# Projections by Strassen's seven products, with intermediates in DRAM, in a hybrid SSD and gMLP layer on one core

## The chip, the cores and the metric

The kernel runs on one core of one Trainium2 chip. The metric is the device time of one execution in microseconds (us). Matmuls run on TensorE (PE), elementwise work on VectorE (DVE), ScalarE (ACT) and GpSimd (POOL); all DMA transfers are issued from the queue of SyncE (SP). Each engine works through its own instructions in the order in which the program holds them.

## The reference, cut to what matters

2048 tokens of width 1024, one layer, all in float32:

```python
h = rms_norm(x, pre_w)
proj = jnp.einsum('bld,dc->blc', h, w_in)               # 1024 -> 6160 columns
u, v, zg, z, xbc, dt_raw = jnp.split(proj, SPLITS, axis=-1)
y_a = spatial_gating(u, v, zg, v_norm_w, v_norm_b, ws, bs, gmlp_norm_w)
y_b = ssd_mixer(xbc, z, dt_raw, conv_w, conv_b, dt_bias, a_log, d_skip, ssd_norm_w)
y = jnp.concatenate([y_a, y_b], axis=-1)                # 2048 columns
...
# spatial_gating: per head and chunk of 128 tokens, u * (W_s v + b) * silu(zg), grouped RMS norm
# ssd_mixer: causal convolution of width 4 over xbc and SiLU, chunked scan with decay,
#   D skip, times silu(z), grouped RMS norm
# then y times w_out (2048 -> 1024), RMS norm, plus x
```

u, v, zg and z have 1024 columns each, xbc 2048, dt 16. The large products are h times w_in and y times w_out.

## The kernel before, in words

The tokens are worked through in four blocks of 512 (`block`, called for b = 0 to 3). For a block, the normalised input is held in SBUF as `hT`, channels on partitions, in two parts: a high part rounded to the format of the fast matmul and a low part, the remainder. Weights are split alike: `load_w` loads 128 rows of a weight unit, ACT makes the high part (L120), and DVE or, every third time, POOL subtracts it for the low part (L123). A product is then three matmuls (`mm3`, L127 to 130): high by high, high by low, low by high.

The projections of a block are cut into units of eight k-steps of 128 channels. A unit has four accumulators in PSUM, one bank each: four units z with 256 columns (the first 272, since dt's 16 columns ride along), four `xbc`, two `v`, two halves of `w_o` for the SSD's part of y, four `uz` (u and zg side by side), and two halves of `w_o` for the gating's part. All but z have 512 columns, so a unit is 8 x 4 x 3 = 96 matmuls. Every block loads all weights again, five k-steps ahead (`LOOK`).

Everything else is a task (`spawn`, `run_tasks`): a generator that emits a piece of work between two k-steps. After an `xbc` unit the task `ssd` does a head group: convolution (POOL L311, then DVE L313 three times), decay matrices `E` read from DRAM by broadcast (DVE L327), their product with C times B (L361), and per chunk of 128 tokens the scan (L364 to L395). `spatial` and `gating` do the gMLP branch. Results stay in SBUF: `hT`, z's gate `zs`, v, and y as `yT`, split again into two parts (L133, L134). The order on each engine comes from a scheduler that works over the emitted program.

Of the kernel before, what the change touches and what calls it, by code (L numbers as in the profile page):

```python
# [10 lines left out]
BF16 = mybir.dt.bfloat16  # L11
# [16 lines left out]
DTC = GC + NH    # columns of the first gate unit: z of group 0, then dt  # L28
# [7 lines left out]
def hybrid_kernel(ctx: ExitStack, tc: tile.TileContext, x, x_t, pre_w, w_v, w_uz, w_xbc, w_z0, w_z,  # L36
                  v_w, v_b, ws_t, bs_t, gn_w, conv_w, conv_b, dt_bias, a_log, d_skip, sn_w,
                  w_o, post_w, out):
    nc = tc.nc
    seq = x.shape[0]  # L40
    nb = seq // T

    const = ctx.enter_context(tc.tile_pool(name="const", bufs=1))
    hpool = ctx.enter_context(tc.tile_pool(name="hpool", bufs=1))
    ypool = ctx.enter_context(tc.tile_pool(name="ypool", bufs=8))
    t4 = ctx.enter_context(tc.tile_pool(name="t4", bufs=8))
    wraw = ctx.enter_context(tc.tile_pool(name="wraw", bufs=4))
# [6 lines left out]
    dram = ctx.enter_context(tc.tile_pool(name="dram", bufs=2, space=DRAM))  # L54
# [43 lines left out]
        # what b and bs add to the gated sum: rowsum(ws) * b + bs  # L98
# [8 lines left out]

    def row_weights(src):
# [76 lines left out]
    h_tiles = {}  # L185
# [512 lines left out]
```

## Time and profile before

| | |
|---|---|
| time, median of 3 runs | 1691.16 us (1688.84 to 1691.71) |
| profiled execution, its span | 1686.8 us |
| PE busy | 1640.3 us, 97% |
| DVE busy | 1030.1 us, 61% |
| ACT busy | 825.5 us, 49% |
| POOL busy | 793.9 us, 47% |
| PE's granted clock, mean | 0.996 of full speed |
| DMA | 191.91 MB, 114 GB/s mean |

The span runs from the first to the last instruction of the profiled execution; the time of a run lies a few us over it. An engine's busy share is an average over stages; a share of 97% means that this engine almost never waits, and the other engines' shares say how much room they have beside it.

### The profile page before, as it was taken

To read this page: it belongs to the slowest core of one execution; us is meant where nothing else is said; L and a number is where in the kernel's file an instruction comes from. 1 tells how busy PE (TensorE), PEld (TensorE's weight loads), DVE (VectorE), ACT (ScalarE), POOL (GpSimd) and SP (SyncE) were. 2 spreads that over 40 slices of the span, in tenths; PEclk is the share of its full clock that TensorE was granted. 3 is DMA by queue.
4 is the path that set the end of the run, shared out by engine and by line. 5 is a ranking of instruction groups with operands and counts; after the bars stand their busy time and mean duration, and the time that the engine had idled before them with its cause. 6 is when DMAs were issued, how large, how long until landed. Compare 5 with 4: busy or idle time off the path is not lost.

```text
span 1686.8 us, 24913 instructions
## 1 busy us (share of the span) xinstructions
PE 1640.3 (97%) x8554; PEld 1395.5 (83%) x8554; DVE 1030.1 (61%) x1938; ACT 825.5 (49%) x1725; POOL 793.9 (47%) x875
## 2 busy tenths in 40 slices
PE   6999999999999999999999999999999999999997
PEld 5888888887888878888788887888878888888886
DVE  5678772346767777234666787724467777862444
ACT  5456644354446654344444565434534556444442
POOL 4457643234546655233545666513344556551333
PEclk9999999999999999999999999999999999999999
DMA  6323443334433343324353334333524324333341
GB/s 225 98 91 97 130 124 112 92 107 134 154 102 91 110 127 124 107 88 138 95 161 104 88 119 132 125 98 90 155 80 156 112 76 124 91 93 106 89 137 70
DMA packets 111471, 191.91 MB, mean 114 GB/s; under 512 B 13552, under 2 KB 30192, under 8 KB 111344
## 3 DMA queue, kind: packets, MB, share of 16 engines
q1 hardware_dynamic: 111344, 190.32, 36.6%
q8 instruction: 67, 1.10, 0.3%
q14 instruction: 60, 0.49, 0.1%
HBM read 181.75 MB, written 8.52 MB: 113 GB/s over the span
## 4 chain that ended last, share of the span: by engine, by line
PE 80%; DVE 11%; POOL 3%; issue 3%; DMA 2%; ACT 2%; SPq 0%; DVEq 0%; POOLq 0%; ACTq 0%
PE acc L128 23%; PE acc L129 23%; PE acc L130 23%; DVE cv_out L313 3%; PE y_ps L378 2%; DVE E L327 2%; PE s_ps L440 2%; PE y_tp L413 2%; DVE h L234 2%; DMA E<-scr 2%; POOL cv_out L311 2%; PE y_ps L381 1%; PE st_ps L383 1%; PE cb_ps L351 1%; DVE w L123 1%
## 5 line engine op out<-in xcount | busy, mean ns | idle before, releaser
L120 ACT ACTIVATE w<-raw 128x512 fp32r<-128x512 f32 (+2 forms) x576 | 330.7, 580 | 477.7 <-PE acc L130 386.8
L123 POOL TENSOR_TENSOR w<-raw,w 128x512 fp32r<-128x512 f32 (+2 forms) x192 | 243.6, 1269 | 478.0 <-ACT w L120 430.3
L128 PE MATMUL acc<-w,hT 128*128 128x512 f32 (+2 forms) x1280 | 453.8, 357 | 4.7 <-ACT v L552 3.2
L130 PE MATMUL acc<-w,hT 128*128 128x512 f32 (+2 forms) x1280 | 451.2, 354 | 0.8 <-POOL hT L236 0.8
L129 PE MATMUL acc<-w,hT 128*128 128x512 f32 (+2 forms) x1280 | 448.2, 350 | 0.0
L123 DVE TENSOR_TENSOR w<-raw,w 128x512 fp32r<-128x512 f32 (+2 forms) x384 | 270.8, 711 | 267.5 <-ACT w L120 265.2
L128 PEld LDWEIGHTS acc<-w,hT 128*128 128x128 f32 x1280 | 244.0, 191 | 35.3 <-ACT v L552 4.5
L129 PEld LDWEIGHTS acc<-w,hT 128*128 128x128 f32 x1280 | 244.1, 191 | 30.1
L130 PEld LDWEIGHTS acc<-w,hT 128*128 128x128 f32 x1280 | 242.8, 190 | 31.2 <-POOL hT L236 1.1
L128 PE MATMUL acc<-hT,w 128*128 128x512 f32 x512 | 203.7, 398 | 0.0
L130 PE MATMUL acc<-hT,w 128*128 128x512 f32 x512 | 202.7, 396 | 0.0
L129 PE MATMUL acc<-w,yT 128*128 128x512 f32 x512 | 201.7, 395 | 0.0
L129 PE MATMUL acc<-hT,w 128*128 128x512 f32 x512 | 201.4, 393 | 0.0
L128 PE MATMUL acc<-w,yT 128*128 128x512 f32 x512 | 195.5, 395 | 0.3
L130 PE MATMUL acc<-w,yT 128*128 128x512 f32 x512 | 193.5, 391 | 0.0
L313 DVE SCALAR_TENSOR_TENSOR cv_out<-cv_raw,cw,cv_out 128x512 f32<-128x512 f32 x192 | 164.8, 888 | 24.1 <-POOL cv_out L311 23.9
L327 DVE TENSOR_SCALAR E<-E,cst 128x128 f32<-128x128 f32 x256 | 105.6, 470 | 67.1 <-DMA E<-scr 67.1
L128 PEld LDWEIGHTS acc<-w,yT 128*128 128x128 f32 x512 | 96.1, 188 | 22.3 <-DVE o L577 1.6
L129 PEld LDWEIGHTS acc<-w,yT 128*128 128x128 f32 x512 | 96.2, 188 | 21.1 <-DVE w L123 1.0
L130 PEld LDWEIGHTS acc<-hT,w 128*128 128x128 f32 x512 | 96.2, 188 | 20.1
L130 PEld LDWEIGHTS acc<-w,yT 128*128 128x128 f32 x512 | 96.3, 188 | 19.6
L128 PEld LDWEIGHTS acc<-hT,w 128*128 128x128 f32 x512 | 96.3, 188 | 19.3 <-ACT zs L542 0.4
(131 smaller groups left out, 2270.9 us busy)
## 6 DMA issues: line engine op xcount, KB each, us to landing
raw<-w_xbc SPq DMA_DIRECT2D x128, 256.0 KB, 2.8
raw<-w_o SPq DMA_DIRECT2D x128, 256.0 KB, 2.6
raw<-w_uz SPq DMA_DIRECT2D x128, 256.0 KB, 2.7
E<-scr SPq DMA_DIRECT2D x64, 256.0 KB, 3.4
raw<-w_v SPq DMA_DIRECT2D x64, 256.0 KB, 2.7
raw<-w_z SPq DMA_DIRECT2D x96, 128.0 KB, 2.0
xt<-x SPq DMA_DIRECT2D x32, 256.0 KB, 3.9
h<-x_t SPq DMA_DIRECT2D x32, 256.0 KB, 3.0
```

What stands on the lines that cost most here:

```text
L120: nc.scalar.activation(w[:, 0, :], raw, AF.Copy)
L123: eng.tensor_tensor(w[:, 1, :], raw, w[:, 0, :], ALU.subtract)
L128: nc.tensor.matmul(dst, lhsT=a_hi, rhs=b_hi, start=first, stop=False)
L129: nc.tensor.matmul(dst, lhsT=a_hi, rhs=b_lo, start=False, stop=False)
L130: return nc.tensor.matmul(dst, lhsT=a_lo, rhs=b_hi, start=False, stop=last)
L234: nc.vector.scalar_tensor_tensor(h, h, pre_c[:, k:k + 1], rb, ALU.mult, ALU.mult)
L311: nc.gpsimd.tensor_scalar(cv, raw[:, 0:T], cw[:, ti, 0:1], cb[:, ti:ti + 1], ALU.mult, ALU.add)
L313: nc.vector.scalar_tensor_tensor(cv, raw[:, j:j + T], cw[:, ti, j:j + 1], cv, ALU.mult, ALU.add)
L327: nc.vector.tensor_scalar(E[:, h, :], E[:, h, :], d["cst"][:, 0, o + h:o + h + 1], 0.0, ALU.subtract, ALU.min)
L378: nc.tensor.matmul(yps[:, h * HD:(h + 1) * HD], lhsT=E[:, h, :], rhs=xdt[:, h * HD:(h + 1) * HD], start=True, stop=True)
L413: nc.tensor.transpose(out=tp[:, c * P:(c + 1) * P], in_=yg[c][:, i * P:(i + 1) * P], identity=ident)
L440: nc.tensor.matmul(sps[:, cc * 256 + i * P:cc * 256 + (i + 1) * P], lhsT=wsT[:, h, :], rhs=v[c][:, h * P:(h + 1) * P], start=True, stop=True)
```

## The change

All 2048 tokens now go through one unit before the next begins. There are eight units of 1024 columns: z, xbc (two), v, uz (two), and the two halves of w_out's rows ("s" for the SSD's part of y, "g" for the gating's part). A unit takes two pairs of token blocks, (2,0) and (3,1), and each pair is a 2 x 2 block product (two blocks of tokens, two halves of 1024 channels, two halves of 1024 columns) done by Strassen's seven products, each of 512 tokens by 512 channels by 512 columns. A product is two steps (halves j of its channels), a step 24 matmuls of 512 columns.

A product's operands are one block or a sum or difference of two. `operand` loads them as 128x1024 tiles, combines two by one instruction of DVE or POOL (L158), and splits into high (ACT L162) and low part (L163); of the two-input instructions every third goes to POOL. A operands are made two steps ahead, B operands three. Sums of token blocks are made in unit 0, stored (`ac`) and read again in the units after. Products accumulate in pairs in the same PSUM banks (`SETS`): `after` takes what is needed out of the banks between the two and recombines the quadrants. Results of units go to DRAM: h (`hd`), zs, raw convolution inputs, v, y, partial outputs. The SSD is one stream of 16 instances (block by head group) that runs beside units 1 to 5 and reads from there; the gating runs in units 4 and 5. dt comes from small fp32 matmuls in `prep`.

```diff
-LOOK = 5         # k-steps that the weights run ahead
+RUN = 1.36
+LOOK_A = 2
+LOOK_B = 3
+PAIRS = ((2, 0), (3, 1))
+PRODS = {
+    "M4": ([(1, 1, 1)], [(1, 1, 0), (-1, 0, 0)]),
+    "M2": ([(1, 1, 0), (1, 1, 1)], [(1, 0, 0)]),
+    "M5": ([(1, 0, 0), (1, 0, 1)], [(1, 1, 1)]),
+    "M3": ([(1, 0, 0)], [(1, 0, 1), (-1, 1, 1)]),
+    "M1": ([(1, 0, 0), (1, 1, 1)], [(1, 0, 0), (1, 1, 1)]),
+    "M7": ([(1, 0, 1), (-1, 1, 1)], [(1, 1, 0), (1, 1, 1)]),
+    "M6": ([(1, 1, 0), (-1, 0, 0)], [(1, 0, 0), (1, 0, 1)]),
+}
+SETS = (("M4", "M2"), ("M5", "M3"), ("M1", "M7"), ("M6",))
...
+    apool = ctx.enter_context(tc.tile_pool(name="apool", bufs=3))
+    bpool = ctx.enter_context(tc.tile_pool(name="bpool", bufs=5))
+    rpool = ctx.enter_context(tc.tile_pool(name="rpool", bufs=6))
+    gpool = ctx.enter_context(tc.tile_pool(name="gpool", bufs=31))
+    qpool = ctx.enter_context(tc.tile_pool(name="qpool", bufs=24))
...
-    def load_w(src, width, name="w"):
-        raw = wraw.tile([P, width], F32, name="raw", tag="raw")
-        nc.sync.dma_start(out=raw, in_=src)
...
+    def operand(pool, name, terms, keep=None):
+        first = rt("r0")
+        nc.sync.dma_start(out=first, in_=terms[0][1])
+        if len(terms) > 1:
+            second = rt("r1")
+            nc.sync.dma_start(out=second, in_=terms[1][1])
+            two_input_engine().tensor_tensor(first, first, second, ALU.add if terms[1][0] > 0 else ALU.subtract)
+            if keep is not None:
+                nc.sync.dma_start(out=keep, in_=first)
+        w = pool.tile([P, 2, 2, T], F32R, name=name)
+        nc.scalar.activation(w[:, :, 0, :], first, AF.Copy)
+        two_input_engine().tensor_tensor(w[:, :, 1, :], first, w[:, :, 0, :], ALU.subtract)
+        return w
...
+            nc.sync.dma_start(out=hd[b][j], in_=h)
...
+                    nc.tensor.matmul(dtp[:, c * NH:(c + 1) * NH], lhsT=h[:, kk, c * P:(c + 1) * P], rhs=wdt[:, k, :],
...
+    def use_v(u):
...
+            s = stage(t, in_psum)
+            nc.vector.bn_stats(vst[b][:, c, n, :], s)
+            nc.sync.dma_start(out=v_d[b][c, :, n * WC:(n + 1) * WC], in_=s)
...
+    UNITS = [("h", use_z(0), False, True), ("h", use_xbc(0), True, True), ("h", use_xbc(1), True, True),
+             ("h", use_v(0), False, True), ("h", use_uz(0), False, True), ("h", use_uz(1), False, True),
+             ("s", use_o0(0), False, True), ("g", use_o1(0), False, False)]
...
+    def make_a(u, p, name, j):
+        kind, terms = UNITS[u][0], PRODS[name][0]
+        if kind == "h" and u > 0 and len(terms) > 1:
+            return operand(apool, "a", [(1, ac[p][name, j])])
+        keep = ac[p][name, j] if kind == "h" and len(terms) > 1 else None
+        return operand(apool, "a", [(s, a_piece(kind, p, m, k, j)) for s, m, k in terms], keep)
...
+    for u, (_, _, _, zigzag) in enumerate(UNITS):
+        if zigzag:
+            order = [(p, s) for s in SETS for p in range(2)]
+        else:
+            order = [(p, s) for p in range(2) for s in SETS]
...
+    def after(u, p, name, c, acc):
...
+        if name == "M4":
+            t["q"] = gt("q_c")
+            nc.scalar.activation(t["q"], acc, AF.Copy)
+        elif name == "M2":
+            t["k"] = gt("k_c")
+            nc.scalar.activation(t["k"], acc, AF.Copy)
+            use(m2, 0, c, t["k"], False)
+        elif name == "M5":
+            nc.vector.tensor_tensor(t["q"], t["q"], acc, ALU.subtract)
+        elif name == "M3":
+            use(m1, 1, c, acc, True)
+            nc.vector.tensor_tensor(t["k"], acc, t["k"], ALU.subtract)
+            nc.gpsimd.tensor_tensor(t["k"], t["k"], t["q"], ALU.add)
+        elif name == "M1":
+            nc.vector.tensor_tensor(t["k"], t["k"], acc, ALU.add)
+        elif name == "M7":
+            nc.vector.tensor_tensor(t["q"], t["q"], acc, ALU.add)
+            use(m1, 0, c, t["q"], False)
+        else:
+            nc.vector.tensor_tensor(t["k"], t["k"], acc, ALU.add)
+            use(m2, 1, c, t["k"], False)
...
+            for kk in range(2):
+                a, b_ = A[:, kk], B[:, kk]
+                st, en = first and j == 0 and kk == 0, j == 1 and kk == 1
+                if channels:
+                    m = mm3(accs[c], b_[:, 0, cs], b_[:, 1, cs], a[:, 0, :], a[:, 1, :], st, en)
+                else:
+                    m = mm3(accs[c], a[:, 0, cs], a[:, 1, cs], b_[:, 0, :], b_[:, 1, :], st, en)
```

In the program before, SP's queue in the first block, while the v units' weights (`raw<-w_v`) are loaded, holds these rows; `xt` is the next block's input and `E` a decay matrix. What stands behind "waits" are semaphores of engines and of DMA queues.

```order
L194 DMA xt<-x 128x512 [waits DVE_49]
L194 DMA xt<-x 128x512 [waits DMAHW6_49,DVE_49]
L324 DMA E<-scr 128x512 [waits DMAHW7_49,PE_49]
L194 DMA xt<-x 128x512 [waits DMAHW0_49,DVE_49]
L118 DMA raw<-w_v 128x512 [waits DMAHW1_49,DVE_49]
L118 DMA raw<-w_v 128x512 [waits DMAHW2_49,DVE_49]
L118 DMA raw<-w_v 128x512 [waits DMAHW3_49,Pool_49]
L324 DMA E<-scr 128x512 [waits DMAHW4_49,PE_49]
```

In the changed program, SP's queue in unit 3 (v), near the end of its products M1 and M7, holds these; `r` are operand loads from weights (`w_u`) or saved sums (`ac`), `vd` the store of v from a recombined quadrant (`q_c`).

```order
L157 DMA r_7217<-w_u 128x1024 [waits DMAHW2_49,Pool_49]
L154 DMA r_7276<-ac0M_108 128x1024 [waits DMAHW3_49,DVE_49]
L154 DMA r_7281<-w_u 128x1024 [waits DMAHW4_49,DMAHW2_49,DVE_49]
L157 DMA r_7283<-w_u 128x1024 [waits DMAHW5_49,Pool_49]
L575 DMA vd_126<-q_c 128x512 [waits DMAHW6_49,DVE_49]
L154 DMA r_7373<-ac0M_109 128x1024 [waits DMAHW7_49,DVE_49]
L379 DMA zs<-zs_122 128x256 [waits DMAHW0_49]
L379 DMA zs<-zs_122 128x256 [waits DMAHW1_49]
L575 DMA vd_126<-q_c 128x512 [waits DVE_49]
L575 DMA vd_126<-q_c 128x512 [waits DMAHW3_49,DVE_49]
L575 DMA vd_126<-q_c 128x512 [waits DMAHW4_49,DVE_49]
L154 DMA r_7460<-ac1M_118 128x1024 [waits DMAHW5_49,Pool_49]
```

Where loads stood among loads, stores that wait for DVE (`vd<-q_c`) now stand between operand loads.

DVE in the first block before, during an SSD task; `w` is a weight's low part:

```order
L364 TENSOR_TENSOR xdt<-xtok,dt 128x256 x2
L123 TENSOR_TENSOR w<-raw,w 128x512
L353 TENSOR_TENSOR cbm<-cb_ps,tri 128x512
L361 TENSOR_TENSOR E<-E,cbm 128x512 x2
L123 TENSOR_TENSOR w<-raw,w 128x256 x2
L364 TENSOR_TENSOR xdt<-xtok,dt 128x256
L390 TENSOR_TENSOR y<-y_ps,xtok 128x256
L393 TENSOR_TENSOR yo<-y_ps,ex 128x256
L388 TENSOR_TENSOR state_106<-state_106,st_ps 128x256
L327 TENSOR_SCALAR E<-E,cst 128x128 x4
```

DVE after, in unit 2 (the second xbc unit), beside the first chunk of an SSD instance; `q_c<-q_c,acc` (L684) takes product M5 out of PSUM, `a` is an A operand's low part:

```order
L414 TENSOR_TENSOR E<-E,cbm 128x512 x2
L684 TENSOR_TENSOR q_c<-q_c,acc 128x512 x2
L372 TENSOR_TENSOR E<-E,cs_863 128x512 x2
L373 TENSOR_SCALAR E<-E 128x512
L684 TENSOR_TENSOR q_c<-q_c,acc 128x512
L373 TENSOR_SCALAR E<-E 128x512
L414 TENSOR_TENSOR E<-E,cbm 128x512
L443 TENSOR_TENSOR y<-y_ps,xtok 128x256
L417 TENSOR_TENSOR xdt<-xtok,dt_311 128x256
L163 TENSOR_TENSOR a<-r_4403,a 128x2x512
L438 COPY state_199<-st_ps 128x256
L414 TENSOR_TENSOR E<-E,cbm 128x512
```

The subtractions from PSUM have come in between the SSD's instructions, and the low parts are now twice as long.

## Rows read from the trace of the kernel before

**Rows 1.** The page: span, busy time by engine, and the DMA queue.

```profile
span 1686.8 us, 24913 instructions
...
PE 1640.3 (97%) x8554; PEld 1395.5 (83%) x8554; DVE 1030.1 (61%) x1938; ACT 825.5 (49%) x1725; POOL 793.9 (47%) x875
...
q1 hardware_dynamic: 111344, 190.32, 36.6%
```

**Rows 2.** Timeline of PE: start us, duration us, what ran, idle before and releaser.

```profile
15.73 0.59 PE L128 MATMUL acc<-w,hT 128*128 128x272 f32 x1 [1.50 <-ACT hT L235]
...
50.00 0.40 PE L129 MATMUL acc<-hT,w 128*128 128x512 f32 x1
...
55.00 0.39 PE L130 MATMUL acc<-hT,w 128*128 128x512 f32 x1
...
55.22 0.28 PE L128 MATMUL acc<-w,hT 128*128 128x256 f32 x1
...
66.73 0.40 PE L128 MATMUL acc<-hT,w 128*128 128x512 f32 x1
...
1676.93 0.39 PE L130 MATMUL acc<-w,yT 128*128 128x512 f32 x1
```

**Rows 3.** Windows: busy us (instructions) by engine, clock, DMA share, GB/s.

```profile
8.00:12.00 4.00, 0.87 (x3) 0.58 (x3) 1.21 (x6) 3.61 (x10) 1.29 (x3) 1.00 1.04 387
...
449.00:453.00 4.00, 4.00 (x19) 3.31 (x18) 2.62 (x8) 2.28 (x7) 0.00 (x0) 1.00 1.04 400
```

**Rows 4.** Groups of instructions, shapes apart: busy us, mean ns | idle before.

```profile
L123 DVE TENSOR_TENSOR w<-raw,w 128x512 fp32r<-128x512 f32 x296 | 222.4, 756 | 229.5 <-ACT w L120 228.2
...
L123 POOL TENSOR_TENSOR w<-raw,w 128x512 fp32r<-128x512 f32 x152 | 211.0, 1388 | 412.7 <-ACT w L120 365.0 <-issue 39.0 <-DMA xt<-x 7.5
...
L120 ACT ACTIVATE w<-raw 128x512 fp32r<-128x512 f32 x448 | 278.3, 626 | 358.8 <-PE acc L130 284.4 <-issue 31.0 <-DMA raw<-w_xbc 30.7
...
L426 DVE SCALAR_TENSOR_TENSOR v<-v,v_mv,row_w 128x1024 f32<-128x1024 f32 x16 | 22.7, 1420 | 0.0
...
L96 POOL TENSOR_TENSOR wsT<-wsT,tri 128x1024 f32<-128x1024 f32 x1 | 2.7, 2673 | 0.0
...
L577 DVE TENSOR_TENSOR o<-o,acc 128x512 f32<-128x512 f32 x32 | 20.4, 682 | 20.9 <-PE acc L130 20.9
...
L313 DVE SCALAR_TENSOR_TENSOR cv_out<-cv_raw,cw,cv_out 128x512 f32<-128x512 f32 x192 | 164.8, 888 | 24.1 <-POOL cv_out L311 23.9
...
L361 DVE TENSOR_TENSOR E<-E,cbm 128x512 f32<-128x512 f32 x64 | 55.5, 887 | 9.2 <-ACT E L329 8.5
...
L390 DVE TENSOR_TENSOR y<-y_ps,xtok 128x256 f32<-128x256 f32 x64 | 26.5, 415 | 3.7 <-PE y_ps L381 1.4 <-PE y_ps L378 0.9
...
L311 POOL TENSOR_SCALAR cv_out<-cv_raw,cw,cb 128x512 f32<-128x512 f32 x64 | 79.8, 1247 | 0.0
...
L395 POOL TENSOR_TENSOR y<-y,zs 128x256 f32<-128x256 f32 x64 | 53.3, 833 | 6.3 <-DVE y L390 3.6
...
L101 PE MATMUL rs_ps<-ones,wsT 128*128 128x2 f32 x16 | 1.8, 246 | 0.0
```

**Rows 5.** Timeline of DVE and POOL at a collision, and of two undisturbed subtractions.

```profile
390.74 7.66 DVE L234 SCALAR_TENSOR_TENSOR h<-h,pre_c,rb 128x512 f32<-128x512 f32 x6
...
392.69 1.74 POOL L236 TENSOR_TENSOR hT<-h,hT 128x512 fp32r<-128x512 f32 x1 [1.29 <-ACT hT L235]
...
394.40 1.74 POOL L123 TENSOR_TENSOR w<-raw,w 128x512 fp32r<-128x512 f32 x1
...
1661.02 0.69 DVE L123 TENSOR_TENSOR w<-raw,w 128x512 fp32r<-128x512 f32 x1 [3.79 <-ACT w L120]
...
1662.47 1.29 POOL L123 TENSOR_TENSOR w<-raw,w 128x512 fp32r<-128x512 f32 x1 [1.59 <-ACT w L120]
```

**Rows 6.** Windows in the middle of blocks, columns as in Rows 3.

```profile
510.00:610.00 100.00, 96.73 (x575) 85.07 (x573) 80.33 (x136) 60.72 (x106) 68.56 (x81) 1.00 0.34 101
...
965.00:985.00 20.00, 18.62 (x133) 17.48 (x132) 17.32 (x31) 12.18 (x22) 16.86 (x22) 1.00 0.31 88
```

More of the change, by code (lines that the diff above doesn't have):

```diff
@@ L18 @@
 T = 512
+NB = 4
 NT = T // P
@@ new lines, in prep @@
+        if b:
+            yield 0
+        rp = bank("r_ps")
+        nc.tensor.matmul(rp, lhsT=ones, rhs=dg.rearrange("p c n -> p (c n)"), start=True, stop=True)
+        rb = gt("rb")
+        nc.vector.tensor_copy(rb, rp)
+        dtp = bank("dt_ps")
+        for j in range(4):
+            h = rt("h")
+            nc.sync.dma_start(out=h, in_=x_t[b, j])
+            for kk in range(2):
+                k = 2 * j + kk
+                nc.vector.scalar_tensor_tensor(h[:, kk, :], h[:, kk, :], pre_c[:, k:k + 1], rb, ALU.mult, ALU.mult)
+            nc.sync.dma_start(out=hd[b][j], in_=h)
+            for kk in range(2):
+                k = 2 * j + kk
+                for c in range(NT):
+                    nc.tensor.matmul(dtp[:, c * NH:(c + 1) * NH], lhsT=h[:, kk, c * P:(c + 1) * P], rhs=wdt[:, k, :],
+                                     start=k == 0 and c == 0, stop=k == KT - 1 and c == NT - 1, skip_group_check=True)
+            if b:
+                yield 0
@@ L240, in hybrid_kernel @@
+        d = sm.tile([P, NG, NT, HG], F32, name=f"dt{b}", bufs=1)
+        bias = hvec[:, 0, :].rearrange("p (g h) -> p g h", g=NG)
+        for c in range(NT):
+            nc.vector.tensor_tensor(d[:, :, c, :], dtp[:, c * NH:(c + 1) * NH].rearrange("p (g h) -> p g h", g=NG),
+                                    bias, ALU.add)
+        spawn(dt_chain(b, d), 20)
     dts = {}
@@ L465, in gating @@
                                         r[:, 2 * c + i:2 * c + i + 1], None, ALU.mult)
-        yield 10
-        yield from y_tiles(yg, 2 * hp, y_out)
-    def finish(b, c, o, ss, xres):
-        r = rsqrt_mean2(ss[:, c:c + 1, :], 1, 1.0 / DM, "o")
-        rows = slice((b * NT + c) * P, (b * NT + c + 1) * P)
-        for n in range(2):
-            h = slice(n * WC, (n + 1) * WC)
-            nc.vector.scalar_tensor_tensor(o[c][:, h], o[c][:, h], r, xres[c][:, h], ALU.mult, ALU.add)
-            nc.sync.dma_start(out=out[rows, h], in_=o[c][:, h])
@@ L621, in hybrid_kernel, with stage @@
-    for b in range(nb):
-        block(b)
-    steps = [(u, k) for u in units for k in range(KT)]
-    loaded = []
-    def load_ahead(n):
-        while len(loaded) < min(n, len(steps)):
-            (src, width, *_), k = steps[len(loaded)]
-            loaded.append(load_w(src[k], width))
+        yield 8
+        yield from y_tiles(b, yg, hp)
+    def stage(t, in_psum, func=AF.Copy):
+        if not in_psum and func == AF.Copy:
+            return t
+        s = gt("stage")
+        nc.scalar.activation(s, t, func)
+        return s
@@ new lines, in make_b @@
+    def make_b(u, name, j):
+        return operand(bpool, "b", [(s, w_u[u, k, n, j]) for s, k, n in PRODS[name][1]])
+    steps = []
+    for u, (_, _, _, zigzag) in enumerate(UNITS):
[3 more added lines that the diff above has]
+            order = [(p, s) for p in range(2) for s in SETS]
+        for p, s in order:
+            for name in s:
+                for j in range(2):
+                    steps.append((u, p, name, j))
+    made_a, made_b = {}, {}
@@ new lines, in hybrid_kernel, with b_key, look_ahead @@
+    looked = [0, 0]
+    def b_key(i):
+        u, p, name, j = steps[i]
+        return (u, name, j) if UNITS[u][3] else (u, p, name, j)
+    def look_ahead(i):
+        while looked[0] < len(steps) and looked[0] <= i + LOOK_A:
+            n = looked[0]
+            made_a[n] = make_a(*steps[n])
+            looked[0] += 1
+        while looked[1] < len(steps) and looked[1] <= i + LOOK_B:
+            n = looked[1]
+            u, p, name, j = steps[n]
+            if b_key(n) not in made_b:
+                made_b[b_key(n)] = make_b(u, name, j)
+            looked[1] += 1
```

557 lines of the change are left out of this document (259 added, 298 removed).

## Prediction, on record before the changed kernel was run

> **What bounds the kernel now.** I read the page's totals first: TensorE (PE) is busy for 1640.3 of 1686.8 us [rows 1], so the kernel ends when its matmuls end. Next the timeline of PE: 22 matmuls of 512 columns lie between 50.00 and 55.00 us, 0.2273 us each, and the 96 matmuls of a 256-column gate unit between 55.22 and 66.73, 11.51 us [rows 2]. The same view shows the ends: 15.73 us before the first projection matmul, 10 us after the last one at 1676.93. The median of the runs, 1691.16, stands 4 us over the span; I add these 4 us to my sums. After these I read, for what the change leans on, the DMA rate where it is full [rows 3], the vector engines' groups by shape [rows 4], a stretch in which VectorE (DVE) and GpSimd (POOL) collide [rows 5], and how much work these two together get done in a dense stretch [rows 6].
>
> **PE: what falls away.** Seven products in place of eight sounds like an eighth of everything, but it is spent on the gate columns. Before, 14 units of 96 matmuls in each of 4 blocks make 5376 matmuls of 512 columns, and 16 gate units (z) come on top. After, 8 units x 28 steps x 24 make 5376 matmuls of 512 columns, z included. So the whole saving is the 16 gate units: 16 x 11.51 = 184 us [rows 2]. Added are 128 small fp32 matmuls for dt; the nearest row, eight fp32 matmuls in 1.8 us (L101 in [rows 4]), gives 0.23 us each, 29 us. PE needs 1640 - 184 + 29 = 1485 us: 8 x 152.7 us of projections (28 x 24 x 0.2273), the dt, and 234 us of small matmuls, which follow the SSD and the gating. By the order of the program that makes 191 us in unit 0, 176, 202, 196, 215, 196 in units 1 to 5, about 156 each in 6 and 7. If PE alone decided, the time would be near 1515 (16 us of start, 10 of tail and 4 outside the span on top). It will not, because of two other prices.
>
> **DMA: what is added.** Every intermediate goes to DRAM and back: 434 MB in 1178 transfers by my count of the program, 190 MB before [rows 1]. Where the queue is full the chip moves 387 to 400 GB/s [rows 3]; the average price of all transfers before is lower, 190.32 MB in 36.6% of the span (617 us), or 308 GB/s [rows 1]. I take 387, from stretches of long transfers in a row, as units 0 and 7 have them, and keep 308 as the other bound. Bytes by unit: 87 MB in unit 0 (x twice, h stored and read, sums of blocks stored, zs stored), 41 to 50 MB in units 1 to 6, 74 MB in unit 7 (weights read for each pair of blocks, partial sums, residual, output). At 387 GB/s 50 MB are 129 us, hidden under 155 us of matmuls. Unit 0: some 10 us until the queue is full (it is at 8 us in [rows 3]), then 38 MB until its first seven steps are fed, 98 us; the other 21 steps hold 49 MB (127 us) but 115 us of matmuls and 29 of dt, about 143: 10 + 98 + 143 = 251 us. Unit 7: 74 MB, 191 us, and 7 until the last operands are split and multiplied: 198 us.
>
> The Trainium skill ("DMA: Bandwidth & Descriptors", Specifications) gives about 358 GB/s as what one core can draw from HBM; the 400 and 387 GB/s in [rows 3] exceed it here. By that figure units 0 and 7 would cost 313 us for 112 MB in place of 289, and the sum would be 24 us longer.
>
> **DVE and POOL: what is added.** This is the term that decides. Each unit of the middle builds 28 A and 14 B operands of 128x1024: 42 low parts and 10 combinations, two thirds on DVE and a third on POOL. Durations, as busy over count [rows 4]: 128x1024 on DVE 1.42 us (L426, the nearest row; twice the 0.75 of L123 says 1.50), on POOL 2.67 (L96; twice 1.39 says 2.78). 35 x 1.42 + 17 x 2.67 = 95 us. The recombination adds 40 DVE additions from PSUM at 0.64 (L577) and 8 POOL additions at 1.39: 37 us. So 132 us a unit that stood nowhere before, against 54 us of L123's 512-column work for the same share of the kernel before ((222.4 + 211.0) / 8, [rows 4]). An SSD instance costs, on DVE, 12 x 0.86 (L313), 8 x 0.87 (L361), 5 x 0.64 and 20 x 0.41 (L390), on POOL 4 x 1.25 (L311) and 21 x 0.83 (L395): 51 us together; a gating instance 12 (at most 20 x 0.41 on DVE and 5 x 0.83 on POOL); the statistics of v 22 (32 at about 0.68, as L577 measures for 512 columns). By the order of the program 2.4, 4.6, 4.2, 3.8 and 1.0 SSD instances lie in units 1 to 5 and 6.5 and 9.5 gating instances in units 4 and 5. The two engines together: 254, 367, 368, 404, 297 us.
>
> How many of these microseconds get done in one? Two would be the most; but the engines collide. At 390.74 six DVE multiplications took 7.66 us, 1.28 each, while POOL's subtractions beside them took 1.74 [rows 5]; undisturbed subtractions of that size take 0.69 and 1.29 (1661.02 and 1662.47). Over 100 us in the middle of a block the two did 80.33 + 68.56, that is 1.49, with PE hardly waiting (96.73); in its densest 20 us 17.32 + 16.86, 1.71, and there PE was down to 18.62 of 20 [rows 6], so that the pair had begun to bind. In units 2 to 4 of the changed kernel it binds throughout. I take 1.71 because that stretch is the one of the same kind, and my loads are on the high side, since neighbouring records overlap a little. Units 1 to 5 are then the larger of PE's time and the load over 1.71: 176, 215, 215, 236, 196 = 1038 us. The bounds are 1.49 below and PE alone above.
>
> **The sum.** 251 + 1038 + 156 (unit 6: PE) + 198 + 10 (tail, as before) = 1653 us of span, 1657 as a time.
>
> **What is hidden, and by what.** ACT has 28 A + 14 B high parts a unit at 1.25 us (twice L120's 0.62, [rows 4]) plus 16 copies from PSUM: some 62 us, and with SSD and gating at most about 150 in a unit; PE covers it, and were the cover gone, ACT would still end before DVE and POOL. The order of the DVE queue shows the price of a collision: an accumulator of the first product of a set must be taken out of PSUM within three chunks, 3 x 1.36 = 4.1 us, before the next product needs the bank; the subtraction that does it (L684) stands among SSD work that waits for DMA and 128x1024 subtractions of 1.4 us. If it is late by more, PE stops, and with it the operands' buffers and so the loads behind them. On SP's queue stores of q_c and v stand ahead of the next operand's load and wait for DVE; before, loads waited only for their own buffer. With operands loaded two to three steps ahead (some 11 to 16 us), a late store costs nothing up to that. In units 0 and 7 the queue is the bound and this cover is gone.
>
> **The rivals.**
> (A, forecast) The pair DVE and POOL binds units 2 to 4 at 1.65 to 1.8: 1623 to 1681, 1657 at 1.71.
> (B, slower) The evacuations and stores that stand in order behind waiting work keep the pair at 1.49 or less, as it was over the 100 us [rows 6]: 176 + 246 + 247 + 271 + 199 = 1139 us, in all about 1758. It decides from 1.63 down: there units 1 to 5 cost 1072, and the sum equals the 1691 of before. For it: in order, more semaphores, four engines in every chain. Against it: in [rows 6] PE was the bound, so the pair had no cause to go faster.
> (C) The pair keeps up, and PE binds the middle: 176 + 202 + 196 + 215 + 196 = 985, 1604 in all. It needs 404 / 215 = 1.88 in unit 4. If instead two-input DVE work and POOL work only took strict turns, a pair of 512-column instructions would go every 1.70 us, as in [rows 5] (POOL starts at 392.69 and 394.40), of which I give 1.15 to POOL and 0.55 to DVE (the undisturbed durations less 0.14 us each): 87 us of turns a unit for operands and recombination and 27.5 an SSD instance, 213 in unit 2, 202 in unit 3, no more than PE elsewhere: 1621. The Trainium skill ("SBUF — State Buffer", Who interferes with whom) has these strict turns as a lock on a shared port; [rows 5] agrees with it.
> (D, slower) Transfers go at the mean price of 308 GB/s, because stores and loads mix in one queue: units 0 and 7 cost 276 and 247, 74 us more, 1731. It decides from 347 GB/s down. For it: waits in SP's queue. Against: [rows 3].
>
> **How the numbers follow.** A 0.45, C with strict turns 0.12, B 0.25, D 0.12, B and D together (about 1830) 0.06. The time is that of A, 1657, its own range 1623 to 1681. Under 1600 I see 3 in 100, over 1785 about 12: the range is 1600 to 1785. Runs of this kernel differ by 0.17%, so 0.2% (3.4 us) is about what can be told from no change. Faster holds A but for its upper edge, C and a little of D: 0.55; the same 0.05; slower 0.40.
>
> **What would show it.** PE's busy time near 1485 and 512-column matmuls unchanged in count; about 434 MB moved, with DMA near full in the first 100 and the last 190 us and about half full between; DVE near 1400 us and POOL near 950 busy; the sum of the two at 1.7 per us from about 430 to 1100 us, with PE at 90% or less there, waiting for operands' low parts or for PSUM; the last unit about 198 us long. The forecast is wrong if DMA stays under 350 GB/s at the ends (D), if the middle shows DVE and POOL at 1.5 or less while PE waits for banks of PSUM (B), or if PE stays at 97% in the middle (C).

## Result, and the profile after

The changed kernel takes 1964.72 us (median of 4 runs, 1959.46 to 1966.6) against 1691.37 us: slower by a ratio of 1.1616, 95% interval 1.1592 to 1.164. The forecast was 1657, its range 1600 to 1785. The profiled execution has a span of 1962.7 us. First the page's totals, which answer to [rows 1].

```profile
span 1962.7 us, 22371 instructions
...
PE 1632.5 (83%) x7268; PEld 1319.5 (67%) x7268; DVE 1476.0 (75%) x2067; ACT 863.1 (44%) x1513; POOL 1073.5 (55%) x754
...
q1 hardware_dynamic: 169376, 434.54, 65.0%
```

PE is no longer nearly always busy: it stands still for 330 us. The bytes are as counted (434.54 MB). No other engine reaches 80%, so the answer must be sought stage by stage. The next windows are the units 0 to 7, each ending with the last recombination of its last product (columns as in [rows 3]).

```profile
0.00:276.00 276.00, 219.74 (x975) 180.96 (x976) 164.09 (x258) 113.52 (x184) 84.57 (x46) 0.93 0.87 313
276.00:482.00 206.00, 184.99 (x844) 150.47 (x843) 156.44 (x191) 92.43 (x131) 117.82 (x81) 0.97 0.69 228
482.00:752.00 270.00, 225.06 (x1036) 183.14 (x1036) 214.15 (x289) 117.62 (x173) 174.93 (x137) 0.91 0.59 193
752.00:1013.00 261.00, 221.29 (x986) 176.04 (x985) 225.16 (x309) 115.10 (x172) 163.03 (x130) 0.92 0.55 184
1013.00:1295.00 282.00, 228.60 (x1079) 186.80 (x1078) 238.55 (x384) 140.32 (x287) 171.88 (x146) 0.90 0.49 159
1295.00:1543.00 248.00, 214.66 (x1020) 177.51 (x1019) 182.70 (x327) 141.03 (x351) 139.15 (x109) 0.90 0.52 171
1543.00:1720.00 177.00, 162.50 (x686) 131.11 (x685) 97.51 (x108) 63.68 (x90) 81.33 (x39) 0.96 0.77 260
1720.00:1946.00 226.00, 175.61 (x653) 133.45 (x652) 185.03 (x185) 77.22 (x122) 134.39 (x65) 0.88 0.82 290
```

Forecast were 251, then 176, 215, 215, 236, 196, then 156 and 198. Units 1 to 5 take 1267 us in place of 1038; that is 229 of the 310 us by which the span missed. In units 2 to 4 DVE and POOL together are busy for 389, 388 and 410 us, close to the loads of the forecast (367, 368, 404), but at 1.44, 1.49 and 1.46 a us, not 1.71. Unit 0 is 25 us over, unit 6 21, unit 7 28, the tail 7.

What PE waits for in units 1 to 5 (276 to 1543 us) shows where it stands still: who waited for what, us in total, times, longest. These are the first rows.

```profile
PE y_ps L431 <- DVE xdt L417: 36.4, 16, 5.0
PE acc L167 <- DVE q_c L684: 19.8, 8, 12.1
PE y_tp L467 <- DVE y L459: 17.7, 8, 3.1
PE xt_tp L390 <- ACT cv_out L348: 12.7, 4, 5.0
PE acc L167 <- DVE k_c L690: 12.6, 6, 5.1
```

All rows together make 192 us; PE is busy for the other 1075. 123 of the 192 stand in front of small matmuls of the SSD and the gating (`y_ps`, `y_tp`, `xt_tp` and others), which wait for a piece that DVE or ACT makes. 45 stand in front of projection matmuls (`acc`) whose bank of PSUM is still being read (`q_c`, `k_c`), and 21 in front of those that wait for an operand. PE takes its matmuls in order, so a late piece of the SSD stops the projections that stand behind it.

How a collision becomes a stop of PE is seen in the timeline around 1848 us, in unit 7 (POOL, DVE and PE, each in order of time; columns as in [rows 2]).

```profile
1848.27 4.62 POOL L163 TENSOR_TENSOR a<-r,a 128x1024 fp32r<-128x1024 f32 x1 [2.56 <-ACT a L162]
...
1848.35 1.22 DVE L163 TENSOR_TENSOR b<-r,b 128x1024 fp32r<-128x1024 f32 x1
1849.49 1.22 DVE L158 TENSOR_TENSOR r<-r,r 128x1024 f32<-128x1024 f32 x1
...
1852.95 0.55 PE L169 MATMUL acc<-b,a 128*128 128x512 f32 x1 [2.59 <-POOL a L163]
1853.30 0.63 PE L167 MATMUL acc<-b,a 128*128 128x512 f32 x1
1853.73 0.63 PE L168 MATMUL acc<-b,a 128*128 128x512 f32 x1
...
1856.93 0.39 PE L168 MATMUL acc<-b,a 128*128 128x512 f32 x1
1857.16 0.62 PE L169 MATMUL acc<-b,a 128*128 128x512 f32 x2
```

POOL's subtraction takes 4.62 us beside two two-input DVE instructions of 1.22 (a low part and a combination), about their time longer than it takes elsewhere (its mean is 2.63, and 2.41 at 1856.44). PE waits 2.59 us for that low part, and then issues its matmuls every 0.43 us in place of 0.23, until 1856.7. The collision goes the other way too:

```profile
548.81 2.37 POOL L163 TENSOR_TENSOR a<-r,a 128x1024 fp32r<-128x1024 f32 x1
...
552.35 2.82 POOL L163 TENSOR_TENSOR b<-r,b 128x1024 fp32r<-128x1024 f32 x1
...
548.88 4.03 DVE L347 SCALAR_TENSOR_TENSOR cv_out<-cv_raw,cw,cv_out 128x512 f32<-128x512 f32 x2 [1.62 <-POOL cv_out L345]
...
552.95 2.76 DVE L347 SCALAR_TENSOR_TENSOR cv_out<-cv_raw,cw,cv_out 128x512 f32<-128x512 f32 x1
...
557.18 1.08 PE L431 MATMUL y_ps<-xdt,E 128*128 128x64 f32 x8 [1.76 <-DVE xdt L417]
```

Three convolution steps of the SSD take 2.0, 2.0 and 2.8 us while POOL subtracts (and, between its two subtractions, multiplies), where one takes 0.75 in a run below that leaves POOL idle. PE then stops for `xdt`, which stood behind them in DVE's queue.

### The profile page after: what moved, and what is told of

It reads as the page before. It is cut to its first block, busy times and chain, and to the rows that moved or that the text cites. A ratio compares the mean times of both kernels' runs of the same rounds, so it can differ in the third digit from the quotient of the medians.

```text
span 1962.7 us, 22371 instructions
## 1 busy us (share of the span) xinstructions
PE 1632.5 (83%) x7268; PEld 1319.5 (67%) x7268; DVE 1476.0 (75%) x2067; ACT 863.1 (44%) x1513; POOL 1073.5 (55%) x754
## 3 DMA queue, kind: packets, MB, share of 16 engines
q1 hardware_dynamic: 169376, 434.54, 65.0%
## 4 chain that ended last, share of the span: by engine, by line
DVE 33%; PE 19%; DMA 18%; POOL 11%; issue 10%; ACT 7%; SPq 2%; DVEq 0%; POOLq 0%; ACTq 0%
DMA r<-w_u 6%; DVE cv_out L347 6%; PE acc L167 5%; PE acc L168 5%; PE acc L169 5%; DVE r L158 4%; DVE a L163 4%; DMA r<-yd 3%; DMA cv_raw<-raw 2%; DVE b L163 2%; POOL r L158 2%; POOL a L163 1%; POOL cv_out L345 1%; DVE E L372 1%; DMA v<-vd 1%
## 5 line engine op out<-in xcount | busy, mean ns | idle before, releaser
L167 PE MATMUL acc<-b,a 128*128 128x512 f32 x1344 | 563.0, 422 | 120.3 <-ACT a L162 35.8
L168 PE MATMUL acc<-b,a 128*128 128x512 f32 x1344 | 549.7, 411 | 2.5 <-POOL b L163 1.3
L169 PE MATMUL acc<-b,a 128*128 128x512 f32 x1344 | 530.0, 409 | 22.1 <-DVE a L163 11.4
L167 PEld LDWEIGHTS acc<-b,a 128*128 128x128 f32 x1344 | 268.1, 200 | 197.1 <-ACT a L162 48.0
L162 ACT ACTIVATE a<-r 128x1024 fp32r<-128x1024 f32 x224 | 235.2, 1053 | 235.0 <-DVE r L158 77.1
L169 PEld LDWEIGHTS acc<-b,a 128*128 128x128 f32 x1344 | 265.6, 198 | 89.9 <-DVE a L163 15.8
L168 PEld LDWEIGHTS acc<-b,a 128*128 128x128 f32 x1344 | 268.6, 200 | 58.6 <-POOL b L163 2.1
L163 DVE TENSOR_TENSOR a<-r,a 128x1024 fp32r<-128x1024 f32 x151 | 214.9, 1425 | 84.4 <-ACT a L162 84.2
L163 POOL TENSOR_TENSOR a<-r,a 128x1024 fp32r<-128x1024 f32 x73 | 191.9, 2629 | 153.1 <-ACT a L162 145.2
L162 ACT ACTIVATE b<-r 128x1024 fp32r<-128x1024 f32 x126 | 132.6, 1054 | 211.3 <-DVE r L158 103.7
L347 DVE SCALAR_TENSOR_TENSOR cv_out<-cv_raw,cw,cv_out 128x512 f32<-128x512 f32 x192 | 211.0, 1119 | 13.6 <-POOL cv_out L345 13.1
L158 DVE TENSOR_TENSOR r<-r,r 128x1024 f32<-128x1024 f32 x102 | 155.6, 1526 | 76.7 <-DMA r<-yd 45.1
L158 POOL TENSOR_TENSOR r<-r,r 128x1024 f32<-128x1024 f32 x48 | 122.2, 2546 | 150.9 <-DMA r<-w_u 79.5
L167 PE MATMUL acc<-a,b 128*128 128x512 f32 x448 | 180.2, 412 | 11.6 <-DVE q_c L684 5.8
L168 PE MATMUL acc<-a,b 128*128 128x512 f32 x448 | 182.2, 407 | 6.9 <-DVE a L163 4.0
L169 PE MATMUL acc<-a,b 128*128 128x512 f32 x448 | 180.6, 405 | 0.0
L163 POOL TENSOR_TENSOR b<-r,b 128x1024 fp32r<-128x1024 f32 x44 | 116.8, 2654 | 113.6 <-ACT b L162 97.7
L163 DVE TENSOR_TENSOR b<-r,b 128x1024 fp32r<-128x1024 f32 x82 | 128.0, 1561 | 66.7 <-ACT b L162 66.6
```

What stands on the lines that cost most here:

```text
L158: two_input_engine().tensor_tensor(first, first, second, ALU.add if terms[1][0] > 0 else ALU.subtract)
L162: nc.scalar.activation(w[:, :, 0, :], first, AF.Copy)
L163: two_input_engine().tensor_tensor(w[:, :, 1, :], first, w[:, :, 0, :], ALU.subtract)
L347: nc.vector.scalar_tensor_tensor(cv, raw[:, j:j + T], cw[:, ti, j:j + 1], cv, ALU.mult, ALU.add)
```

## Experiments

The theories. **V**: the work of DVE and POOL, which includes their collisions, sets the time. **Q**: the work would fit, but operands and SSD pieces come late because of short look-ahead and of what stands ahead in the queues. **K**: PE itself is the bound, since its clock falls after stops. Later expectations add **S**: ScalarE's queue holds up the operands' high parts. Every run is one execution, unless said otherwise; the kernel before, run beside each, had medians of 1689 to 1693 us.

**Two matmuls in place of three**

```diff
-        nc.tensor.matmul(dst, lhsT=a_hi, rhs=b_lo, start=False, stop=False, skip_group_check=True)
-        return nc.tensor.matmul(dst, lhsT=a_lo, rhs=b_hi, start=False, stop=last, skip_group_check=True)
+        return nc.tensor.matmul(dst, lhsT=a_lo, rhs=b_lo, start=False, stop=last, skip_group_check=True)
```

> Each step of the projections does two matmuls in place of three (high by high, and low by low in place of the two mixed ones, so that every operand part is still built and read; the output lacks the mixed terms). PE's projections fall from 1222 to 815 us. Theory V (the work of VectorE and GpSimd is the bound) and theory Q (operands and SSD pieces come late because of the order in the queues and short look-ahead): the time hardly falls, 1850 to 1965 us. Theory K (PE itself is the bound, since its clock falls after each stall): about 400 us less, 1560.

Measured 1866.64 us. A third of the projections' matmuls is gone, 407 us at full clock, and the time falls by 98, not by the 400 of K. K falls; for the most part PE follows others.

**Operand work on DVE alone, or half on POOL**

```diff
-        return nc.gpsimd if turn[0] % 3 == 0 else nc.vector
+        return nc.vector
```

The second run has `turn[0] % 2` there.

> All combinations and low parts of operands on VectorE, none on GpSimd. V as the sum of both engines: their work falls by 165 x (2.63 - 1.43) = 198 us, at 1.45 a us 137 us less, about 1830. V with VectorE alone as the bound: its work rises by 236 us, 2000 to 2150. Q: the chain of a third of the operands is 1.2 us shorter, 1900 to 1950.

> Half of the operands' two-input work on GpSimd in place of a third. V as the sum: 83 instructions cost 1.2 us more each, 100 us of work, about 2030. V with VectorE alone as the bound: 119 us less on it, about 1850. Q: longer chains, 1970 to 2010.

Measured 1842.27 and 2016.85 us, near V's 1830 and 2030; with DVE's own length as the bound the signs would have been the other way round. The groups of DVE by shape show why. First the changed kernel, then the one with operand work on DVE alone:

```profile
L163 DVE TENSOR_TENSOR a<-r,a 128x1024 fp32r<-128x1024 f32 x151 | 214.9, 1425 | 84.4 <-ACT a L162 84.2
L347 DVE SCALAR_TENSOR_TENSOR cv_out<-cv_raw,cw,cv_out 128x512 f32<-128x512 f32 x192 | 211.0, 1119 | 13.6 <-POOL cv_out L345 13.1
L417 DVE TENSOR_TENSOR xdt<-xtok,dt 128x256 f32<-128x256 f32 x64 | 49.0, 766 | 8.3 <-ACT xtok L393 8.3
L684 DVE TENSOR_TENSOR q_c<-q_c,acc 128x512 f32<-128x512 f32 x64 | 42.1, 676 | 3.3 <-PE acc L169 3.3
```

```profile
L163 DVE TENSOR_TENSOR a<-r,a 128x1024 fp32r<-128x1024 f32 x224 | 289.5, 1294 | 65.9 <-ACT a L162 65.7
L347 DVE SCALAR_TENSOR_TENSOR cv_out<-cv_raw,cw,cv_out 128x512 f32<-128x512 f32 x192 | 167.9, 892 | 13.8 <-POOL cv_out L345 13.7
L417 DVE TENSOR_TENSOR xdt<-xtok,dt 128x256 f32<-128x256 f32 x64 | 31.5, 492 | 3.2 <-ACT xtok L393 3.2
L684 DVE TENSOR_TENSOR q_c<-q_c,acc 128x512 f32<-128x512 f32 x64 | 42.2, 676 | 1.7 <-PE acc L169 1.7
```

And the page's totals with operand work on DVE alone:

```profile
PE 1587.9 (86%) x7268; PEld 1297.9 (71%) x7268; DVE 1467.3 (80%) x2252; ACT 877.9 (48%) x1523; POOL 633.8 (34%) x569
```

DVE does 165 more operand instructions and is busy for 9 us less (1467.3 against 1476.0); POOL sheds 440. At 1.29 us each the 165 alone would be 213 us more, so more than 200 of DVE's busy microseconds had been waits for POOL. Instructions with two inputs in SBUF shrink (1119 to 892 ns, 766 to 492), the one that reads one input from PSUM does not (676, 676). A multiplication by one factor per partition, with a single tensor as input, shrinks too:

```profile
L541 DVE TENSOR_SCALAR y<-y,g_r 128x128 f32<-128x128 f32 x128 | 44.0, 413 | 2.0 <-POOL g_r L175 2.0
```

```profile
L541 DVE TENSOR_SCALAR y<-y,g_r 128x128 f32<-128x128 f32 x128 | 30.4, 306 | 1.9 <-POOL g_r L175 1.9
```

The first is of the changed kernel, the second of the other. The Trainium skill ("SBUF — State Buffer", Who interferes with whom) says that VectorE and GpSimd share one pair of ports under an exclusive lock, that a VectorE instruction with two inputs in SBUF contends there with GpSimd's reads, and that `tensor_scalar` can do so in its two-port modes. These rows agree, though none shows in which mode L541 ran.

**Stores from ScalarE's queue**

```diff
-            nc.sync.dma_start(out=y_d[b][j][:, i, :], in_=yT)
+            nc.scalar.dma_start(out=y_d[b][j][:, i, :], in_=yT)
```

Likewise for the other tiles that ScalarE makes.

> Stores of tiles that ScalarE has made (y, zs, and the parts of raw, v and partial outputs that it copies) are issued from ScalarE's own queue, not from SyncE's, where they stood ahead of loads and waited. V: no change, within 1% of 1965. Q by SyncE's queue: the waits of SyncE for ScalarE (about 290 us of its time) go, operands come earlier, 1800 to 1900.

Measured 1960.93 us: no change. SP's waiting stores of what ScalarE makes cost nothing that matters; those of what DVE makes stayed on SP.

**More look-ahead**

```diff
-        while looked[0] < len(steps) and looked[0] <= i + LOOK_A:
+        while looked[0] < len(steps) and looked[0] <= i + LOOK_A + (1 if i >= 28 else 0):
```

Likewise for LOOK_B.

> From unit 1 on, operands are made one step earlier (A three steps ahead, B four), with a fourth A and a sixth B buffer; the pool of 512-column tiles shrinks from 31 to 24 to make room. Q (operands come late for want of look-ahead): 1800 to 1880 us. V (the amount of work of VectorE and GpSimd): 1950 to 1990.

Measured 1981.71 us, as V had it. The smaller pool may hide a gain.

**Without the SSD**

```diff
-            yield from conv(b, g, res)
-            yield from ssd(b, g, res)
+            for i in range(2):
+                t = gt("yT")
+                nc.sync.dma_start(out=t, in_=raw_d[g][i][:, b * T:(b + 1) * T])
+                nc.sync.dma_start(out=y_d[b][4 + g][:, i, :], in_=t)
+            yield 30
```

> The SSD stream is left out: two convolution inputs per instance are copied to DRAM in place of its result, so the output lacks the convolution, the scan, the gate z and the norm of that branch. V: units 1 to 3 hold 132 us of VectorE and GpSimd work each and units 4 and 5 some 217 to 249, so the first fall to about 160, the others to 165 and 190: about 1530 us in all. Q: the projections alone keep their own stalls, every unit stays at 190 or more, over 1650.

Measured 1555.26 us. Units 1 to 3 of it as windows:

```profile
272.00:425.00 153.00, 152.81 (x675) 126.21 (x674) 80.59 (x80) 60.94 (x73) 56.30 (x26) 1.00 0.82 278
425.00:584.00 159.00, 155.09 (x676) 127.62 (x675) 74.40 (x76) 55.84 (x67) 58.16 (x26) 0.99 0.77 259
584.00:748.00 164.00, 157.14 (x691) 129.00 (x690) 96.44 (x129) 56.95 (x70) 57.15 (x28) 0.99 0.75 253
```

With the SSD away, the same operands, loads, stores and evacuations leave PE busy nearly throughout, at 153 to 164 us a unit, where the matmuls alone need 152.7. So in these units the machinery of the seven products does not stall by itself, only beside the SSD. Units 0, 6 and 7, where no SSD instance lies by the forecast's count, take 272, 176 and 224 us here, almost as long as in the changed kernel. Of the 409 us saved less than 234 can be matmuls of the SSD's own, since that was the forecast's count of all small matmuls, the gating's among them.

**Low parts of A stored once, and the convolution's first step on ScalarE** (both on the kernel with operand work on DVE)

```diff
-        two_input_engine().tensor_tensor(w[:, :, 1, :], first, w[:, :, 0, :], ALU.subtract)
+        if lo_in is None:
+            two_input_engine().tensor_tensor(w[:, :, 1, :], first, w[:, :, 0, :], ALU.subtract)
+        if lo_out is not None:
+            nc.sync.dma_start(out=lo_out, in_=w[:, :, 1, :].bitcast(F32))
...
-            nc.gpsimd.tensor_scalar(cv, raw[:, 0:T], cw[:, ti, 0:1], cb[:, ti:ti + 1], ALU.mult, ALU.add)
+            nc.scalar.activation(cv, raw[:, 0:T], AF.Identity, scale=cw[:, ti, 0:1], bias=cb[:, ti:ti + 1])
```

> On top of the kernel with all operand work on VectorE (1842 us): unit 1 stores the low parts of the A operands, units 2 to 5 load them in place of subtracting. VectorE loses 112 subtractions of 1.29 us, 144 us; DMA gains 14.7 MB in unit 1 and 14.7 MB in each of four units. V: 100 to 144 us less, 1700 to 1740. Q: only the subtraction's own latency goes, 1800 to 1840. If DMA binds in the middle (508 MB at 340 GB/s): no gain or a loss, 1840 or more.

> The last one and, beside it, the first multiplication of the convolution on ScalarE in place of GpSimd (64 instructions of 1.49 us, during which VectorE's two-input instructions wait). V by collisions on GpSimd and VectorE: 30 to 60 us below the last run. Q: within 15 us of it.

Measured 1791.38 and 1761.23 us. The first gains 51 us, about half of the least that V forecast; the second 30, the least that V had. The prices of V are too high here: what is taken off DVE comes back only in part.

**GpSimd emptied, and its two halves**

```diff
-            nc.vector.tensor_tensor(E, E, d["cs"][:, o:o + HG].unsqueeze(2).broadcast_to([P, HG, P]), ALU.subtract)
-            nc.vector.tensor_scalar(E, E, 0.0, None, ALU.min)
-            nc.scalar.activation(E, E, AF.Exp)
+            for h in range(HG):
+                nc.scalar.activation(E[:, h, :], E[:, h, :], AF.Relu, scale=-1.0, bias=d["cs"][:, o + h:o + h + 1])
+            nc.scalar.activation(E, E, AF.Exp, scale=-1.0)
...
-            nc.gpsimd.tensor_tensor(y, y, zs[c], ALU.mult)
+            nc.vector.tensor_tensor(y, y, zs[c], ALU.mult)
```

Likewise for the norm factors (to ScalarE) and for GpSimd's other two-input work (to VectorE).

> On top of the last kernel (1761 us): the decay's subtraction and minimum and the two multiplications by a norm's factor go from VectorE to ScalarE (some 160 us less on VectorE, 140 more on ScalarE), and all two-input work that GpSimd still had (some 480 us there) goes to VectorE, where it costs about 200. V by collisions: with GpSimd gone, VectorE's instructions run undisturbed, VectorE stays near 1310 us, and units 1 to 5 come within 5% of PE's own 985 us plus the clock's share: 1660 to 1700. If GpSimd's help was worth more than its collisions: VectorE binds, 1760 or more. Q: within 15 us of 1761.

> Half of the run that gave 1805 us, on top of the kernel of 1761 us: only the moves from VectorE to ScalarE (decay's subtraction and minimum, two norm factors); GpSimd keeps its work. V (amount on VectorE and GpSimd): 160 us less on VectorE, 1700 to 1740. If ScalarE's queue is now what holds up the operands' high parts (theory S): 1780 or more.

> The other half: GpSimd's two-input work goes to VectorE, ScalarE as in the kernel of 1761 us. If collisions cost more than GpSimd's help: 1720 to 1750. If VectorE's length of queue binds (theory V with VectorE alone): 1790 or more. S: within 15 us of 1761.

Measured 1805.48 with both, 1786.14 with ScalarE's part, 1810.58 with VectorE's part, all above 1761.23. V as an amount of work falls here; the times expected of longer queues on ScalarE (S) and on VectorE came true. The page's totals of the kernel of 1761 and of the one with GpSimd emptied are

```profile
PE 1562.7 (89%) x7268; PEld 1279.7 (73%) x7268; DVE 1327.0 (75%) x2140; ACT 892.3 (51%) x1565; POOL 509.3 (29%) x505
```

```profile
PE 1574.4 (87%) x7268; PEld 1288.5 (71%) x7268; DVE 1290.2 (72%) x2260; ACT 1035.9 (57%) x2019; POOL 76.9 (4%) x65
```

DVE and POOL together lost 469 us of busy time, and the time rose by 44. The collisions are gone (a convolution step takes 750 ns, 877 in the kernel of 1761 us), but the work now stands in two queues, each in order, and more of it on ScalarE (+25 us alone) or on VectorE (+49 alone) costs time, though neither engine is full. In unit 2 of the kernel with GpSimd emptied the pair is busy for 172 of 249 us:

```profile
455.00:704.00 249.00, 220.73 (x1022) 180.70 (x1021) 166.93 (x322) 158.39 (x291) 4.62 (x4) 0.91 0.78 272
```

PE's waits in units 1 to 5 say what came late. In front of small matmuls they grow from 47 us (kernel of 1761) to 60, 90 and 81 (ScalarE's part, VectorE's part, both); for operands they are 22, then 26, 19 and 15. So it is pieces of the SSD and the gating that come late, more than the operands that S named.

**Look-ahead again, and a last unit that reads its weights once** (on the kernel of 1761 us; the second edit, with three more 512-column tiles, also on the one with GpSimd emptied)

```diff
-             ("s", use_o0(0), False, True), ("g", use_o1(0), False, False)]
+             ("s", use_o0(0), False, True), ("g", use_o1(0), False, True)]
```

> On the kernel of 1761 us: from unit 1 on A operands three and B operands four steps ahead, with one more buffer of each; the pool of 512-column tiles has 26 in place of 31. If what is left over PE's own time in the middle (1117 against 985 us) is operands that come late for want of look-ahead (Q): 1690 to 1730. If it is the length of the queues of VectorE and ScalarE between SSD work and operands (S, V): 1750 to 1785.

> The last one with the last unit's two pairs of blocks taken in turns, as in the other units, so that its 24 weight blocks are read once: 12.6 MB less in a unit that moves 74 MB. If DMA binds the last unit (it is busy for 92% of it at 332 GB/s): 20 to 35 us less, less a longer tail of up to 10. If the recombination and the final sums on VectorE bind it: no gain.

> The kernel of 1761 us with the last unit's two pairs of blocks taken in turns (12.6 MB less there) and three more 512-column tiles. By DMA as the bound of the last unit: 10 to 15 us less, as in the run beside the kernel without GpSimd, about 1748; still slower than the 1691 us of the kernel before.

Look-ahead: 1784.24 us, 23 more, in the range of S and V. Units 6 and 7 got shorter (161 us after 174, 191 after 197), units 1 to 5 together longer (1154 after 1117, the most in unit 2, 260 after 237). PE's waits for operands there fell from 22 us to 11, those in front of small matmuls rose from 47 to 82. So want of look-ahead costs some 20 us in the last two units and little beside the SSD; that the smaller pool of 26 tiles made the SSD later is likely but not shown, since no run had more look-ahead with an equal pool. The last unit: 1798.58 against 1805.48, and 1752.91 (4 runs, 1751.26 to 1758.04) against 1761.23. These 7 and 8 us are less than the expected 20 to 35 and 10 to 15: in the second the unit's last matmuls end 33 us sooner (164 us after 197), but the tail behind them is 22 longer (37 after 15). The ratio of the second to the kernel before is 1.0373, interval 1.0353 to 1.0392. It is the best version found; none of those that compute everything beats the kernel before.

## Why the prediction was wrong

**The step that failed** is "In units 2 to 4 of the changed kernel it binds throughout", with the rate that follows: "I take 1.71 because that stretch is the one of the same kind, and my loads are on the high side". They gave 1038 us for units 1 to 5, which took 1267. Measured are 1.30 to 1.49 a us, with loads up to 8% above the forecast. The step was wrong in kind and not only in size. Busy time of DVE and POOL is no amount of work that could be divided by a rate, because each engine's records contain its waits for the other: a third of the operands on POOL in place of none put over 200 us into DVE's busy time. And a unit does not end when the pair's load is done: with GpSimd emptied the pair fills 172 of unit 2's 249 us, and the kernel is no faster. Nor does the 1.71 of [rows 6], read as the pair having "begun to bind", show a bound. PE's whole idle time in that stretch (965 to 985 us of the kernel before) is one wait:

```profile
PE y_ps L381 <- DVE state L388: 1.4, 1, 1.4
```

**What the runs show in its place**: the middle is PE's own time and PE's stops, and most of the stops are small matmuls that wait for a piece of the SSD or the gating. The operand work went to where the SSD already was, and made the SSD's own instructions longer (the convolution step from 888 ns in [rows 4] to 1119). Units 1 to 5 by run, in us:

| kernel | units 1 to 5 | PE busy | idle before small matmuls | idle for operands or banks |
|---|---|---|---|---|
| changed | 1267 | 1075 | 123 | 66 |
| 1842: operand work on DVE alone | 1200 | 1054 | 96 | 49 |
| 1761: less work on both, fewer collisions | 1117 | 1031 | 47 | 38 |
| 1786: that of 1761 with more on ScalarE | 1141 | 1037 | 60 | 43 |
| 1811: that of 1761 with GpSimd's work on VectorE | 1167 | 1040 | 90 | 36 |
| 1805: that of 1761 with both moves | 1164 | 1040 | 81 | 42 |
| 1784: that of 1761 with more look-ahead | 1154 | 1041 | 82 | 30 |

**Rival B** (DVE and POOL at 1.49 or less), with a chance of 0.25, had the right rate for units 2 to 4, and its mechanism, late evacuations and stores, in part only: 45 of PE's 192 us of waits were for banks of PSUM, and the stores that were moved cost nothing. It was under-priced at 1758: it had 1139 us for units 1 to 5, 79 of the difference in units 1 and 5 (206 and 248 in place of 176 and 199, at 1.33 and 1.30 a us), and it left units 0, 6 and 7 as forecast, which took 74 us more together.

**PE's term** held in its projections: 5376 matmuls, 152.7 us a unit, as the run without SSD shows (153 in unit 1). PE is busy for 147 us beyond the 1485; 70 of these are matmuls at the lower clock after its stops (351 of 5189 distances between projection matmuls are about 0.43 us in place of 0.23), which the sum had at nothing, and 11 are dt's matmuls (40.5 us in place of 29). The rest was not split.

**DMA's term** was small in error. With operand work off POOL, units 0 and 7 take 258 and 196 us, near the 251 and 198; in the changed kernel 276 and 226:

```profile
0.00:258.00 258.00, 215.66 (x975) 179.46 (x976) 166.88 (x283) 114.14 (x185) 22.95 (x21) 0.94 0.92 335
1630.00:1826.00 196.00, 157.95 (x650) 124.70 (x648) 179.61 (x231) 77.36 (x122) 32.66 (x20) 0.95 0.92 334
```

So 18 of unit 0's 25 us and all of unit 7's 28 go when the operand work leaves POOL. The start of unit 0 was as forecast: PE's first projection matmul comes late, at 46.67 us, but the seventh step starts at 108.29, where the sum had 10 + 98. The excess lies behind it:

```profile
108.29 0.48 PE L167 MATMUL acc<-b,a 128*128 128x512 f32 x1
```

At a DMA share of 0.92 the 335 GB/s would be about 364 if full (an estimate), not 387; stores stand among the loads there, though no run shows that they are the reason. The Trainium skill's 358 GB/s ("DMA: Bandwidth & Descriptors", Specifications), against which the forecast held the full stretches of [rows 3], is nearer for this mix. Rival D has a slip: at 308 GB/s the second 49 MB of unit 0 are 159 us, more than the 143 of PE, so D comes to 1747 and not 1731.

**What was called hidden** was hidden in part. The stores of what ScalarE makes were (no change when moved). ACT's high parts cost PE 5 us of waits in units 1 to 5, but 27 in unit 7. The evacuation of PSUM is nearly hidden in units 1 to 3 without the SSD (PE is idle there for 11 of 476 us) and costs 45 us in units 1 to 5 of the changed kernel.

**What stays open**: in the kernel of 1761 us units 1 to 5 still take 1117 us, 132 above PE's 985: 46 of longer PE time and 86 of stops, with DVE busy for 83% of a unit at most. Moving work to ScalarE or to VectorE made the stops longer, so the order in these two queues seems to decide there; that is argued from these runs. No run changed the order alone, and none moved the SSD's matmuls further back in PE's queue, where a late piece would stop less.

## What to carry to other kernels

Before counting an engine's idle time as room, ask what its neighbour's instructions would do to the ones already there: two-input work on GpSimd costs its own duration and, here, half as much again in waits on VectorE (440 and over 200 us), so try the split with none on GpSimd first, and then with a little. Do not add up two engines' busy times as if they were work. Ask also which instructions of the bottleneck engine stand behind which waits: here most stops of PE were small matmuls of another task, not the products themselves. A product saved on TensorE that must be paid with additions on already busy engines has to be priced in the densest stage, and with the other stages' work lying there. A test that takes away the neighbour (here the SSD) tells in one run whether new machinery stalls by itself.

## What was not expected of the hardware

After a stop of 2.59 us (1852.95) PE's clock stood at 0.54 of full on the mean from 1853.0 to 1856.5, so at its lower level of 1.2 GHz for most of that stretch, where matmuls of 512 columns came every 0.43 us; from 1857 it was at 1.00 (clock, DMA share and GB/s end each row):

```profile
1853.00:1856.50 3.50, 3.50 (x9) 2.76 (x10) 0.00 (x0) 1.54 (x2) 0.06 (x1) 0.54 0.97 337
1857.00:1861.00 4.00, 4.00 (x19) 3.31 (x18) 2.89 (x2) 2.11 (x4) 4.00 (x2) 1.00 1.00 360
```

Over the kernel the mean is 0.916 against 0.996 before, 0.822 with a third of the matmuls left out: in these three runs, the more PE waits, the slower it then works.
